# Sample's mixture heads: keys copied by residue inside each 512 tokens, local scores over a border in two pieces, prompt heads prepared one ahead

## The chip, the cores and the metric

The kernel runs on one core of a Trainium2 chip. The metric is device time in microseconds (us) of one execution, the median of several runs. PE is TensorE, DVE VectorE, ACT ScalarE, POOL GpSimd; SP (SyncE) issues nearly all DMAs here, in order, from one queue.

## The reference, cut to what matters

One encoder layer is run on two requests with shared weights, a prompt of 512 tokens and a sample of 1024, width 1024, all in float32. The part that the change touches is the token mixer's first eight heads ("mixture a"):

```python
qa, ka, va, qb, kb, vb = jnp.split(x @ w_in, splits, axis=-1)
qa = rotary(qa.reshape(B, T, 8, 64)); ka = rotary(ka.reshape(B, T, 8, 64))
oa = dilated_mixture_attention(qa, ka, va)   # windows (128, stride 1), (512, 4), (2048, 16), mixed by their lse
ob = neighbourhood_attention(qb, kb, vb, rpb)
y = concat([rms_norm(oa, g_mix_a), rms_norm(ob, g_mix_b)]) @ w_out
```

After it come cross-attention into 256 memory tokens and a squared-ReLU MLP, each with a residual sum and a layer norm.

## The kernel before, in words

Every float32 product is made of fp32r parts: a value is split in a high part and a rest, and a product takes three matmuls of up to 512 columns (`mm3`, L129 to L131).

The mixer's work is written as a list of 32 heads: eight a heads and eight b heads of the prompt, then eight a and eight b of the sample. A pair of heads shares its weights. A head is prepared by `qk_a` or `qk_b` for each 512 tokens (the group g): 24 matmuls project q and k into bank `pj`, DVE and POOL turn them (L383 to L386), ACT and DVE split them (L387, L388), and `stack` lays high and rest in the layout that the scores read, by SP's DMAs. The first head of a pair also projects v (24 matmuls for each group) and begins with the pair's weights, which SP loads (L92) and ACT and POOL split (L320, L321, L106, L107).

A prepared head is then attended in units of four blocks of 128 queries: the prompt has one unit a head, a sample a head four (two over near keys, two over every fourth key, "dilated"). `unit` is a generator of four steps: scores into bank `s` (L502, L503) with bias, maximum and exp on DVE and ACT; transposes of the probabilities (L528) and their split; the products with v into the one bank `o` (L544), which ACT empties (L550); the transposes back (L554). `push` puts a new unit in front and takes one step of each unit that is open, so four units overlap. `attend` walks the heads and hands out, between their units, the preparation of later heads: `lead(j)` is the head k during which head j is prepared, j - 2 for the prompt and j - 1 for the sample. What is written in this order a scheduler then places on each engine, so the instructions of neighbouring units and preparations stand mixed; `order`'s rows below are that final order.

For the sample's a heads, `stack` first writes k and q a second time, with the tokens sorted by their residue modulo 4, into a pair of tiles that all heads share (`env["perm"]`, tag `gb`; ACT L359 makes the high part, POOL L360 the rest). The next group's sort can begin when the DMAs that read the pair have landed. The head tile `hd` holds q as it is, k twice and q sorted, 1024 tokens each; k and the sorted q lie in four residue rows of 256 tokens, so a group of 512 tokens fills half of each row: a DMA moves four runs of 128 elements a partition (L368 to L370), a plain q one run of 512 (L366).

Layer norm of the sample's second 512 tokens (`ln_in` 8 to 11) with its load (L228), store (L230) and transposes (L137) stands with the first heads' preparation, ahead of the first `push`. `xs` is the layer-normed input in memory, `x0` (the prompt), `x1` and `x2` (the sample) are its parts as matmul operands.

Of the kernel before, what the change touches and what calls it, by code (L numbers as in the profile page):

```python
# [21 lines left out]
P = 128  # L22
# [9 lines left out]
def f32(ap):  # L32
    return ap.bitcast(F32)
# [3 lines left out]
def tile_encoder_layer(ctx: ExitStack, tc: tile.TileContext, d, outs):  # L37
    nc = tc.nc
    V, A, G, T, S = nc.vector, nc.scalar, nc.gpsimd, nc.tensor, nc.sync
# [21 lines left out]
    def slot(tag, n=None, dt=F32):  # L61
        w, bufs = SLOT[tag]
        t = sb.tile([P, w], dt, name=tag, tag=tag, bufs=bufs)
        return t if n is None else t[:, 0:n]
# [6 lines left out]
    def bank(tag):  # L71
        return ps.tile([P, 512], F32, name=tag, tag=tag, bufs={"t": 3, "o": 1}.get(tag, 2))
# [172 lines left out]
    z = slot("tok", 620)  # L245
# [3 lines left out]
    z = slot("tok", 465)  # L249
# [13 lines left out]
    call = lambda f, *a: (lambda: f(*a))  # L263
# [6 lines left out]
    def mixer(r, fill):  # L270
# [75 lines left out]
        def by_residue(a):  # L346
            return a.rearrange("p (x q) -> p q x", q=4)

        def residues(a):
            return a.rearrange("p (q x) -> p q x", q=4)  # L350

        def stack(hd, sh, sl, g):

            qs, k1, k2 = hd[0:3]
            tt = slice(g * 512, (g + 1) * 512)
            kh, kl = sh, sl
            if r:
                kh, kl = env["perm"]
                A.activation(residues(kh), by_residue(f32(sh)), AF.Copy)  # L359
                G.tensor_copy(residues(kl), by_residue(f32(sl)))  # L360
                kh, kl = residues(kh), residues(kl)
                k1, k2, qp = (residues(k)[:, :, g * P:(g + 1) * P] for k in hd[1:4])
            else:
                k1, k2 = k1[:, tt], k2[:, tt]
            for o, x, y, z in ((slice(0, 64), sh, kh, kl), (slice(64, P), sl, kl, kh)):
                S.dma_start(f32(qs[o, tt]), f32(x[0:P:2]))  # L366
                if r:
                    S.dma_start(f32(qp[o]), f32(y[0:P:2]))  # L368
                S.dma_start(f32(k1[o]), f32(y[1:P:2]))
                S.dma_start(f32(k2[o]), f32(z[1:P:2]))  # L370

        def head_tile(is_b):
            t = act.tile([P, 4096], F32R, name="hd", tag="act")
            return tuple(t[:, i * 1024:(i + 1) * 1024] for i in range(3 if is_b else 4))
# [95 lines left out]
        def unit(hd, v, h, blocks, norm=None, then=None, scale=1.0, local=False):  # L470
# [3 lines left out]
            qs, k1, k2 = hd[0:3]  # L474
# [3 lines left out]
            s, sx, pr, x = None, 512, None, 512  # L478
# [10 lines left out]
            for i, (q, kc, bias, n, lead, width, chunks) in enumerate(blocks):  # L489
                if sx + n > 512:  # L490
                    soften()
                    s, sx = bank("s"), 0
                if x + width > 512:
                    pr, x = slot("q", 512), 0
                so, p = s[:, sx:sx + n], pr[:, x + lead:x + lead + n]
                if lead:
                    G.memset(pr[:, x:x + lead], 0.0)
                if lead + n < width:
                    G.memset(pr[:, x + lead + n:x + width], 0.0)
                probs.append(pr[:, x:x + width])  # L500
                sx, x = sx + n, x + width
                T.matmul(so, q(qs), kc(k1), start=True, stop=False, skip_group_check=True)  # L502
                T.matmul(so, q(qs), kc(k2), start=False, stop=True, skip_group_check=True)  # L503
                todo.append((i, so, p, bias))
            soften()
            yield
# [16 lines left out]
            for pk in packs:  # L523
                t = bank("t")
                x = 0
# [9 lines left out]
            o = None  # L535
            for pk, (hi, lo) in zip(packs, split):
                if o is None:
                    o = bank("o")
                x = 0
                for c, u in pk:  # L540
                    n = len(u) * P
                    q0 = u[0][0] * P
                    for part in (hi, lo):
                        T.matmul(o[:, q0:q0 + n], v(c, h), part[:, x:x + n],  # L544
                                 start=(done == 0 and part is hi), stop=(done == total - 1 and part is lo),
                                 skip_group_check=True)
# [5 lines left out]
            t = bank("t").rearrange("p (i h e) -> p i h e", i=4, h=2)  # L552
# [20 lines left out]
        cols = lambda a, n, s=1: (lambda z: z[:, a:a + (n - 1) * s + 1:s])  # L573
# [5 lines left out]
        def attn_a1(hd, v, h, tab, hg):  # L579
            for j in range(2):  # L580
                bl = []
                for b in range(4 * j, 4 * j + 4):
                    lead, n = (64, 192) if b == 0 else (0, 192) if b == 7 else (0, 256)
                    k0 = (b * P - 64 + lead) // 4
                    bl.append((cols(b * P, P), lambda z, k0=k0, n=n: residues(z)[:, :, k0:k0 + n // 4],
                               tab[:, lead:lead + n], n, lead, 256, (b, (b + 1) % 8)))

                def then(raw, j=j):
                    S.dma_start(oas[0][j * 512:(j + 1) * 512, hg].rearrange("(i p) c -> p i c", p=P), raw)
                push(unit(hd, v, h, bl, then=then, local=True))  # L590
                yield
            for j in range(2):
                bl = []
                for q in (2 * j, 2 * j + 1):
                    for i in range(2):
                        bl.append((cols(q * 256 + i * P, P), cols(q * 256, 256),
                                   tab[:, 384 - P * i:640 - P * i], 256, 0, 256, (8 + 2 * q, 9 + 2 * q)))

                def then(raw, j=j):
                    for i in range(2):  # L600
                        S.dma_start(oas[1].rearrange("(h p q) g c -> q p h g c", p=P, q=4)[2 * j + i, :, :, hg],
                                    raw[:, 2 * i:2 * i + 2])
                push(unit((hd[3],) + hd[1:3], v, h, bl, then=then))
                yield
# [102 lines left out]

        return [x for is_b in (False, True) for pair in range(4) for x in pair_ab(pair, is_b)]

    def attend(heads, lead, after=()):  # L710

        for k, (_, units, n) in enumerate(heads):
            work = [f for j in range(len(heads)) if lead(j) == k for f in heads[j][0]]
            if k == len(heads) - 1:
                work += after
            us, done = units(), 0
            for i in range(n):
                next(us)
                while done < len(work) * (i + 1) // n:
                    work[done]()  # L720
                    done += 1
            for _ in us:
                pass
# [9 lines left out]
    def merge(t):  # L733
# [15 lines left out]
        for i in range(2):  # L749
# [2 lines left out]
        V.tensor_add(o, o, t[1][:, :, 0:64])  # L752
        S.dma_start(os_[1][rows, 0:512].rearrange("p (g c) -> p g c", g=8), o)

    plan = mixer(0, []) + mixer(1, [None] * 36 + [call(merge, t) for t in range(8)] +
                                [call(tok_load, 0, t) for t in range(4)])


# [162 lines left out]
            for f in extra.get((h, 1), ()):  # L921
                f()

    for f in plan[0][0] + [call(ln_in, 8)] + plan[1][0] + [call(ln_in, i) for i in range(9, 12)]:
        f()
    attend(plan, lambda j: j - 2 if j < 16 else j - 1, [call(y_tile, 0, t) for t in range(4)])
    while pipe:
        step()
    w_out_half(0, 0)
# [154 lines left out]
    for n, i in enumerate(UP):  # L1084
        _, what, into = PRODUCTS[i]
        xs_ = lefts.pop(n)
        for f in range(16):
# [3 lines left out]
            o = bank(("pj", "s", "t")[f % 3])  # L1091
# [9 lines left out]
            b = {2: (0, 1), 7: (1, 0), 6: (1, 1)}.get(i)  # L1101
# [176 lines left out]
```

## Time and profile before

| | |
|---|---|
| runs | 2379.81, 2386.12, 2386.31 us (median 2386.12) |
| the profiled execution | 2380.81 us, of which its trace spans 2379.0 |
| PE busy | 2284.5 us (96%), 11124 matmuls |
| DVE, ACT, POOL busy | 68%, 43%, 37% of the span |
| mean granted PE clock | 0.990 |

In the trace the prompt's heads run from about 134 to 345 us, the sample's a heads to about 650, its b heads and the rest of the mixer's end to about 990, the cross-attention and the MLP up to 2379. PE works in the order of its own queue, so a matmul whose operand is late holds all behind it; an idle stretch of PE carries the name of what ended it.

### The profile page before, as it was taken

What the parts mean: (1) busy time and instruction counts of PE and PEld (TensorE: products, weight loads), DVE (VectorE), ACT (ScalarE), POOL (GpSimd) and SP (SyncE); (2) the same over time, 40 slices, a digit from 0 to 9 for tenths busy, and PEclk for the clock granted to TensorE, in tenths of its full rate; (3) what the DMA queues carried; (4) which work ended last, traced back from release to release, by engine and by line L of the source; (5) the groups of instructions that cost most, each with busy time, mean ns of one, the idle gap of its engine ahead of it and who ended that gap; (6) DMA issues with size and microseconds to landing.
All of it is one profiled execution on the core that took longest, in us unless ns stands there. A gap on an engine that the chain in (4) does not pass through costs nothing. (4 is left out here: it accounts for less than half of the span.)

```text
span 2379.0 us, 33108 instructions
## 1 busy us (share of the span) xinstructions
PE 2284.5 (96%) x11124; PEld 1892.7 (80%) x11124; DVE 1608.6 (68%) x3297; ACT 1022.7 (43%) x2176; POOL 879.3 (37%) x820
## 2 busy tenths in 40 slices
PE   8989998999999999999999999999999999999997
PEld 6868777888888787777878877878888888887875
DVE  6265635677656667668676487767776696689786
ACT  4345645666555532334333333333354322344541
POOL 7564443223324211433154355555541314310221
PEclk9999999999999999999999999999999999999998
DMA  9675345677535642435335444344489999974781
GB/s 318 201 228 146 78 117 121 137 137 150 116 95 135 180 124 92 133 115 176 117 107 185 121 155 147 120 139 147 149 223 221 210 222 250 224 177 156 165 206 68
DMA packets 410235, 375.21 MB, mean 158 GB/s; under 512 B 72513, under 2 KB 326481, under 8 KB 410065
## 3 DMA queue, kind: packets, MB, share of 16 engines
q1 hardware_dynamic: 367056, 339.54, 49.7%
q0 software_dynamic: 43008, 33.56, 10.1%
q8 instruction: 88, 1.44, 0.3%
q14 instruction: 83, 0.67, 0.1%
HBM read 290.76 MB, written 52.98 MB: 144 GB/s over the span
## 5 line engine op out<-in xcount | busy, mean ns | idle before, releaser
L107 POOL TENSOR_TENSOR wl<-wraw,wh 128x512 fp32r<-128x512 f32 x80 | 106.2, 1344 | 218.5 <-ACT wh L106 169.3
L1062 ACT ACTIVATE wh<-q 128x512 fp32r<-128x512 f32 x176 | 110.1, 626 | 140.5 <-DMA q<-in_w_up_dram 61.5
L486 ACT ACTIVATE q<-q,st 128x256 f32<-128x256 f32 (+3 forms) x256 | 138.4, 544 | 60.3 <-DVE st L485 59.0
L1063 DVE TENSOR_TENSOR wh<-q,wh 128x512 fp32r<-128x512 f32 x176 | 125.8, 717 | 54.2 <-ACT wh L1062 53.9
L321 POOL TENSOR_TENSOR wl<-wraw,wh 128x256 fp32r<-128x256 f32 x128 | 94.0, 757 | 160.3 <-ACT wh L320 144.9
L1047 POOL DMA_DIRECT2D q<-in_w_up_dram x64 | 83.3, 1416 | 181.0 <-DVE h L1100 72.8
L532 DVE TENSOR_TENSOR pt<-t,pt 128x512 fp32r<-128x512 f32 x160 | 105.2, 670 | 54.8 <-ACT pt L531 54.0
L1047 POOL DMA_DIRECT2D q<-in_w_down_dram x64 | 56.4, 921 | 218.9 <-DVE wraw L1134 92.9
L1000 POOL TENSOR_TENSOR wl<-pt,wh 128x512 fp32r<-128x512 f32 x64 | 91.6, 1451 | 118.6 <-ACT wh L999 118.4
L544 PE MATMUL o<-pt,tok 128*128 128x256 f32 (+3 forms) x576 | 116.1, 315 | 9.1 <-ACT q L550 8.6
L531 ACT ACTIVATE pt<-t 128x512 fp32r<-128x512 f32 x160 | 89.6, 579 | 80.1 <-PE o L544 76.4
L107 POOL TENSOR_TENSOR wl<-qt,wh 128x512 fp32r<-128x512 f32 x64 | 101.6, 1608 | 51.3 <-ACT wh L106 43.4
L1013 DVE TENSOR_TENSOR tok<-tok,t 128x512 f32<-128x512 f32 x124 | 82.9, 680 | 37.5 <-PE t L131 37.4
L1013 DVE TENSOR_TENSOR tok<-tok,s 128x512 f32<-128x512 f32 x124 | 83.8, 679 | 29.7 <-PE s L131 29.4
L131 PE MATMUL pj<-x20h,wl 128*128 128x512 f32 x256 | 101.4, 396 | 2.5 <-POOL wl L107 2.3
L119 POOL TENSOR_TENSOR wl<-wraw,wh 128x512 fp32r<-128x512 f32 x48 | 64.7, 1366 | 103.7 <-ACT wh L118 103.7
L129 PE MATMUL pj<-x20h,wh 128*128 128x512 f32 x256 | 100.6, 393 | 1.0 <-ACT wh L106 0.9
L528 PE MATMUL t<-ident,q 128*128 128x128 f32 x624 | 97.9, 276 | 3.3 <-ACT q L486 1.8
L158 POOL TENSOR_TENSOR lnst<-lnst,mhalf 128x1 f32<-128x1 f32 x44 | 54.2, 1234 | 124.7 <-DVE lnst L157 124.6
L130 PE MATMUL pj<-x20l,wh 128*128 128x512 f32 x256 | 100.2, 391 | 0.0
L544 PEld LDWEIGHTS o<-pt,tok 128*128 128x128 f32 x576 | 85.0, 192 | 16.5 <-ACT q L550 11.3
L999 ACT ACTIVATE wh<-pt 128x512 fp32r<-128x512 f32 x64 | 36.9, 624 | 121.7 <-PE s L131 103.2
(497 smaller groups left out, 7527.9 us busy)
## 6 DMA issues: line engine op xcount, KB each, us to landing
q<-in_w_up_dram SPq DMA_DIRECT2D x128, 256.0 KB
q<-in_w_down_dram SPq DMA_DIRECT2D x128, 256.0 KB
wraw<-in_w_in_dram SPq DMA_DIRECT2D x96, 256.0 KB
qt<-in_w_up_dram SPq DMA_DIRECT2D x32, 512.0 KB
pt<-in_w_down_dram SPq DMA_DIRECT2D x32, 512.0 KB
q<-in_w_up_dram POOLq DMA_DIRECT2D x64, 256.0 KB, 8.1
q<-in_w_down_dram POOLq DMA_DIRECT2D x64, 256.0 KB, 5.9
sa<-kv SPq DMA_DIRECT2D x28, 512.0 KB
```

The source lines that it names most:

```text
L107: G.tensor_sub(wl[:, sl], r, f32(wh[:, sl]))
L129: T.matmul(out, lh[k], rh[k], start=(k == 0), stop=False, skip_group_check=True)
L130: T.matmul(out, lh[k], rl[k], start=False, stop=False, skip_group_check=True)
L131: T.matmul(out, ll[k], rh[k], start=False, stop=(k == n - 1), skip_group_check=True)
L486: A.activation(p, p, AF.Exp, bias=nm, scale=scale, accum_out=den)
L528: T.transpose(t[:, x:x + P], p, ident)
L532: V.tensor_sub(lo[:, 0:x], t[:, 0:x], f32(hi[:, 0:x]))
L544: T.matmul(o[:, q0:q0 + n], v(c, h), part[:, x:x + n], start=(done == 0 and part is hi), stop=(done == total - 1 and part is lo), skip_gro ...
L1013: V.tensor_add(x, x, q)
L1047: G.dma_start(out, src, accum_op=ADD)
L1062: A.activation(dst[0], x, AF.Copy)
L1063: low.tensor_sub(dst[1], x, f32(dst[0]))
```

## The change

Four edits.

- In `stack` the sorted k and q of a group stay together: each group fills one run of 512 elements a partition, residue by residue inside it. k's copies are issued ahead of q's.
- A local block of the sample reads keys from 64 tokens ahead of its 128 queries to 64 behind. Blocks 3 and 4 of each head reach over token 512, where the layout now breaks, so their scores are made in two pieces: 48 and 16 keys of each residue. Each piece has its own matmuls (for k1 and for k2).
- A dilated block reads its 128 queries as one run, its keys as two runs of 128.
- `attend` prepares every head during the one ahead of it, and `ln_in` 8 to 11 becomes the filling of the prompt's first pushes (`fill`, after a first empty place).

```diff
         def stack(hd, sh, sl, g):
 
-            qs, k1, k2 = hd[0:3]
+
             tt = slice(g * 512, (g + 1) * 512)
+            qs, k1, k2 = (a[:, tt] for a in hd[0:3])
             kh, kl = sh, sl
             if r:
                 kh, kl = env["perm"]
                 A.activation(residues(kh), by_residue(f32(sh)), AF.Copy)
                 G.tensor_copy(residues(kl), by_residue(f32(sl)))
-                kh, kl = residues(kh), residues(kl)
-                k1, k2, qp = (residues(k)[:, :, g * P:(g + 1) * P] for k in hd[1:4])
-            else:
-                k1, k2 = k1[:, tt], k2[:, tt]
             for o, x, y, z in ((slice(0, 64), sh, kh, kl), (slice(64, P), sl, kl, kh)):
-                S.dma_start(f32(qs[o, tt]), f32(x[0:P:2]))
-                if r:
-                    S.dma_start(f32(qp[o]), f32(y[0:P:2]))
                 S.dma_start(f32(k1[o]), f32(y[1:P:2]))
                 S.dma_start(f32(k2[o]), f32(z[1:P:2]))
+                S.dma_start(f32(qs[o]), f32(x[0:P:2]))
+                if r:
+                    S.dma_start(f32(hd[3][o, tt]), f32(y[0:P:2]))
...
-                T.matmul(so, q(qs), kc(k1), start=True, stop=False, skip_group_check=True)
-                T.matmul(so, q(qs), kc(k2), start=False, stop=True, skip_group_check=True)
+                for dst, keys in kc if local else [(lambda z: z, kc)]:
+                    T.matmul(dst(so), q(qs), keys(k1), start=True, stop=False, skip_group_check=True)
+                    T.matmul(dst(so), q(qs), keys(k2), start=False, stop=True, skip_group_check=True)
...
-                    k0 = (b * P - 64 + lead) // 4
-                    bl.append((cols(b * P, P), lambda z, k0=k0, n=n: residues(z)[:, :, k0:k0 + n // 4],
-                               tab[:, lead:lead + n], n, lead, 256, (b, (b + 1) % 8)))
+                    kc, k0, end = [], b * P - 64 + lead, b * P - 64 + lead + n
+                    for g in range(2):
+                        x0, x1 = max(k0, 512 * g) // 4, min(end, 512 * g + 512) // 4
+                        if x0 < x1:
+                            kc.append((lambda z, a=x0 - k0 // 4, e=x1 - k0 // 4: residues(z)[:, :, a:e],
+                                       lambda z, g=g, a=x0 - P * g, e=x1 - P * g:
+                                       residues(z[:, 512 * g:512 * g + 512])[:, :, a:e]))
...
-                        bl.append((cols(q * 256 + i * P, P), cols(q * 256, 256),
+                        bl.append((cols(512 * i + q * P, P),
+                                   lambda z, q=q: z.rearrange("p (g x) -> p g x", g=2)[:, :, q * P:(q + 1) * P],
...
-    def attend(heads, lead, after=()):
+    def attend(heads, after=()):
 
         for k, (_, units, n) in enumerate(heads):
-            work = [f for j in range(len(heads)) if lead(j) == k for f in heads[j][0]]
-            if k == len(heads) - 1:
-                work += after
+            work = heads[k + 1][0] if k + 1 < len(heads) else after
...
-    plan = mixer(0, []) + mixer(1, [None] * 36 + ...
+    plan = mixer(0, [None] + [call(ln_in, i) for i in range(8, 12)]) + mixer(1, [None] * 36 + ...
...
-    for f in plan[0][0] + [call(ln_in, 8)] + plan[1][0] + [call(ln_in, i) for i in range(9, 12)]:
+    for f in plan[0][0]:
         f()
-    attend(plan, lambda j: j - 2 if j < 16 else j - 1, [call(y_tile, 0, t) for t in range(4)])
+    attend(plan, [call(y_tile, 0, t) for t in range(4)])
```

The scheduler's order changes with it. On PE the rows are the same up to the 511th and from about the 4,280th of some 10,070 on (from about 138 to 990 us of the trace); between them 25 rows more stand in another order. Lines of the changed kernel are 2 to 3 lower in `stack` and `unit`: L363 and L364 copy k, L365 and L367 q, L500 and L501 make scores, L406 and L454 transposes of v, L526 of probabilities.

The first place is PE at the first a head of the sample (`hd_3552`). `s_3756` holds the scores of blocks 2 and 3, of which block 3 is the first to read keys of the second 512 tokens; `pj_3693` is the projection of v for the second 512 tokens, 24 matmuls. Before:

```order
L457 MATMUL pj_3684<-ident_92,kv_3676 128x128 x4
L554 MATMUL t_3798<-ident_92,q_3508 128x128 x2
L528 MATMUL t_3839<-ident_92,q_3744 128x128 x3
L502 MATMUL s_3756<-hd_3552 128x256
L503 MATMUL s_3756<-hd_3552 128x256
L502 MATMUL s_3814<-hd_3552 128x256
...
L503 MATMUL s_3814<-hd_3552 128x256
L129 MATMUL pj_3693<-x2h_1141,wh_3641 128x512
L130 MATMUL pj_3693<-x2l_1142,wh_3641 128x512
```

And now, with 24 rows of `pj_3693` between the two parts:

```order
L500 MATMUL s_3756<-hd_3552 128x4x48
L501 MATMUL s_3756<-hd_3552 128x4x48
...
L500 MATMUL s_3816<-hd_3552 128x4x16
L501 MATMUL s_3816<-hd_3552 128x4x16
L526 MATMUL t_3843<-ident_92,q_3744 128x128
L129 MATMUL pj_3693<-x2h_1273,wh_3641 128x512
...
L131 MATMUL pj_3693<-x2h_1273,wl_3642 128x512
L500 MATMUL s_3756<-hd_3552 128x4x16
L501 MATMUL s_3756<-hd_3552 128x4x16
```

Before, the scores over the second group's keys stood ahead of v's projection; now only the pieces over the first group's keys do, and the piece over the second group's (4x16) stands behind it.

The second place is SP's queue at the start of the prompt's heads: `wraw` is a half of pair 1's weights, `tok_1143` the sample's tokens for `ln_in` 8, `tok_1209` and `tok_1235` those for 9 and 10, `tok_1026` and `tok_1027` tiles of the prompt's second head. Before:

```order
L370 DMA tok_1026<-qt_1084 64x512
L228 DMA tok_1143<-in_x_sample_dram 128x1024
L380 DMA kv_1194<-in_c_rope_dram 128x2x512
L92 DMA wraw_1337<-in_w_in_dram 128x4x128
L92 DMA wraw_1343<-in_w_in_dram 128x4x128
...
L230 DMA xs1_58<-tok_1143 128x1024
L366 DMA tok_1026<-qt_1196 64x512
...
L228 DMA tok_1209<-in_x_sample_dram 128x1024
L228 DMA tok_1235<-in_x_sample_dram 128x1024
```

And now:

```order
L365 DMA tok_1025<-qt_1084 64x512
L377 DMA kv_1196<-in_c_rope_dram 128x2x512
L92 DMA wraw_1321<-in_w_in_dram 128x4x128
L92 DMA wraw_1327<-in_w_in_dram 128x4x128
...
L92 DMA wraw_1671<-in_w_in_dram 128x4x128
L363 DMA tok_1027<-qt_1198 64x512
L364 DMA tok_1027<-qt_1198 64x512
```

The loads and stores of `ln_in` have left the place; weights stand there, also a first load of pair 2 (`wraw_1671`), ahead of the second head's copies.

## Rows read from the trace of the kernel before

**Rows 1.** The page, busy time of each engine, share of the span, instructions.

```profile
PE 2284.5 (96%) x11124; PEld 1892.7 (80%) x11124; DVE 1608.6 (68%) x3297; ACT 1022.7 (43%) x2176; POOL 879.3 (37%) x820
```

**Rows 2.** Windows by stage: stretch, its us, busy by engine, PE clock, DMA.

```profile
134.00:180.00 46.00, 38.51 (x175) 29.70 (x175) 36.74 (x73) 24.35 (x50) 31.08 (x26) 0.93 0.78 233
180.00:345.00 165.00, 157.17 (x827) 130.06 (x827) 85.92 (x268) 98.13 (x251) 78.43 (x113) 0.99 0.44 111
345.00:650.00 305.00, 287.93 (x1758) 252.63 (x1757) 200.79 (x655) 182.96 (x499) 89.21 (x118) 0.98 0.64 133
650.00:990.00 340.00, 327.49 (x1722) 277.57 (x1722) 224.56 (x588) 158.18 (x359) 99.68 (x113) 0.99 0.45 126
```

**Rows 3.** PE's waits, 345 to 650: us in total, times, longest us.

```profile
PE s L502 <- DMA hd<-gb: 9.3, 5, 5.6
PE o L544 <- ACT q L550: 4.9, 3, 1.9
```

**Rows 4.** PE's waits, 134 to 180.

```profile
PE t L137 <- POOL tok L173: 2.6, 2, 1.7
PE pj L129 <- ACT wh L106: 1.4, 1, 1.4
PE pj L129 <- ACT wh L320: 1.3, 1, 1.3
```

**Rows 5.** PE's waits, 180 to 345.

```profile
PE o L544 <- ACT q L550: 3.3, 3, 2.7
```

**Rows 6.** Windows at a low granted clock (0.50, third number from the end).

```profile
141.00:144.40 3.40, 3.40 (x9) 2.64 (x8) 0.55 (x1) 2.30 (x6) 3.40 (x3) 0.50 0.60 189
164.90:168.30 3.40, 3.40 (x13) 2.90 (x13) 2.89 (x9) 3.40 (x8) 3.40 (x5) 0.50 0.88 282
380.40:383.40 3.00, 2.94 (x10) 2.65 (x11) 2.10 (x9) 0.00 (x0) 0.00 (x0) 0.51 0.20 51
```

**Rows 7.** Timelines of PE, ACT and SP at the sample's first head.

```profile
363.53 0.39 PE L131 MATMUL pj<-x2h,wl 128*128 128x512 f32 x1
363.76 0.39 PE L129 MATMUL pj<-x1h,wh 128*128 128x512 f32 x1
...
370.86 1.13 ACT L359 ACTIVATE gb<-qt 128x512 fp32r<-128x512 f32 x1 [2.77 <-DMA hd<-gb]
...
376.25 0.61 SPq L369 DMA_DIRECT2D hd<-gb  x1
...
380.46 0.58 PE L502 MATMUL s<-hd 128*128 128x256 f32 x1 [5.61 <-DMA hd<-gb]
```

**Rows 8.** Timelines of SP and PE at a b head: L402 copies 64x1024.

```profile
821.82 0.47 SPq L402 DMA_DIRECT2D hd<-hd  x1
...
825.12 0.57 PE L502 MATMUL s<-hd 128*128 128x256 f32 x2 [0.87 <-DMA hd<-hd]
```

**Rows 9.** Timelines of SP and PE at the sample's second head.

```profile
422.12 0.62 SPq L369 DMA_DIRECT2D hd<-gb  x1
...
427.16 0.36 PE L502 MATMUL s<-hd 128*128 128x256 f32 x1 [1.37 <-DMA hd<-gb]
```

**Rows 10.** Timeline of PE: starts of scores of 256 and 192 columns.

```profile
388.15 0.28 PE L503 MATMUL s<-hd 128*128 128x256 f32 x1
388.27 0.25 PE L502 MATMUL s<-hd 128*128 128x192 f32 x1
388.36 0.28 PE L503 MATMUL s<-hd 128*128 128x192 f32 x1
```

**Rows 11.** Timelines of SP and ACT: pair 1's second half of weights.

```profile
131.62 1.09 SPq L92 DMA_DIRECT2D wraw<-in_w_in_dram  x2
...
137.30 1.64 ACT L320 ACTIVATE wh<-wraw 128x256 fp32r<-128x256 f32 x4 [8.36 <-DMA wraw<-in_w_in_dram]
```

**Rows 12.** Timelines of PE and SP: a prompt b head's projection and last copy.

```profile
347.86 0.39 PE L131 MATMUL pj<-x0h,wl 128*128 128x512 f32 x1
...
352.24 0.52 SPq L403 DMA_DIRECT2D tok<-tok  x1
```

More of the change, by code (lines that the diff above doesn't have):

```diff
@@ L583, in attn_a1 @@
                     lead, n = (64, 192) if b == 0 else (0, 192) if b == 7 else (0, 256)
-                    k0 = (b * P - 64 + lead) // 4
-                    bl.append((cols(b * P, P), lambda z, k0=k0, n=n: residues(z)[:, :, k0:k0 + n // 4],
-                               tab[:, lead:lead + n], n, lead, 256, (b, (b + 1) % 8)))
+                    kc, k0, end = [], b * P - 64 + lead, b * P - 64 + lead + n
[5 more added lines that the diff above has]
+                                       residues(z[:, 512 * g:512 * g + 512])[:, :, a:e]))
+                    bl.append((cols(b * P, P), kc, tab[:, lead:lead + n], n, lead, 256,
+                               (b, (b + 1) % 8)))
                 def then(raw, j=j):
@@ L753, in merge @@
         S.dma_start(os_[1][rows, 0:512].rearrange("p (g c) -> p g c", g=8), o)
-    plan = mixer(0, []) + mixer(1, [None] * 36 + [call(merge, t) for t in range(8)] +
+    plan = mixer(0, [None] + [call(ln_in, i) for i in range(8, 12)]) + mixer(1, [None] * 36 + [call(merge, t) for t in range(8)] +
                                 [call(tok_load, 0, t) for t in range(4)])
```

## The prediction

> **What bounds the kernel now.** I read the page's busy times first: PE works 96% of the span [rows 1], so only what PE waits for, how fast its clock runs and how many matmuls it has can change the time. Then the windows by stage, to see where PE is not busy. The two built programs have PE's same rows up to about 138 us and again from about 990 us, so all that can move lies in the four stages of [rows 2]: there PE is idle 7.5 us of 46, 7.8 of 165, 17.1 of 305 and 12.5 of 340. That is 45 us in all, and no edit can win more than that and what the clock loses beside it.
>
> The waits tell whose idle time it is. In the sample's a heads 9.3 us of the 17.1 end with a copy of keys into the head tile, five waits, one of 5.6 [rows 3]; the next, 4.9, is bank `o` waiting for ACT to empty it, which no edit touches by itself. At the start of the prompt's heads PE waits 2.6 us for the layer norm of the sample's second half, and 2.7 for split weights [rows 4]; in that stretch DVE is busy 36.7 and POOL 31.1 of 46 us and the DMA engines 0.78, the highest share of the four [rows 2]. In the rest of the prompt the largest wait is bank `o` again [rows 5].
>
> The clock is the last view. It fell to 0.50 (1.2 of 2.4 GHz) in three stretches of these stages that the change can reach [rows 6]. A stretch of 3.4 us in which PE worked at half speed cost 1.7 us, twice; the third held 2.94 us of work, 1.5 us lost. Each came within or right after waits of PE: the last behind the 5.6 us.
>
> **The copies by residue.** At the sample's first head the projection of q and k for the second 512 tokens ends at about 363.8, and the scores that read its keys begin at 380.46, held for 5.61 us: 16.7 us from projection to keys [rows 7]. Part of it is the shared pair of tiles: ACT's sort of the second group begins at 370.86, after 2.77 us of waiting for the first group's copies to land. Then the last copy is issued at 376.25 and lands 4.2 us later. At the second head the last copy takes 5.0 us (422.12 to 427.16) [rows 9]. These copies are of 512-byte runs. The nearest row of long runs is a b head's copy of 64x1024, twice the bytes in 4 KB runs: 821.82 to 825.12, 3.3 us [rows 8]. So a landing should come 0.9 to 1.7 us sooner, and it lies on the path twice, once before the sort and once before the scores: 1.8 to 3.4 us of 16.7, of which I take 2.6. The lower bound is nothing.
>
> What PE does meanwhile matters as much. I counted the rows between the end of the second group's projection and the first score over its keys, at the start-to-start times of the trace: 0.23 us for 512 columns [rows 7], 0.12 for 256 [rows 10], 0.11 for a transpose. Before, the eight heads have 10.1, 16.5, 23.3, 16.5, 23.3, 16.5, 23.3, 16.5 us of PE work there; now 15.5, 16.2, 24.1, 14.7, 15.3, 15.6, 15.9, 14.9. The first head gains because 24 matmuls of v (5.5 us) stand ahead of the waiting piece now. Its 5.6 us become about 1.2: 16.7 less 15.5, or by the other view a transpose that now stands 1.5 us behind its scores where it stood 2.2 before. The other four waits share 3.7 us (9.3 less 5.6), so the second heads of a pair needed about 16.5 + 0.9 = 17.4 us. With 2.6 less they need 14.8, and 16.2, 14.7, 15.6 and 14.9 leave next to nothing; I take 1.0 for all. So 9.3 us become 2.2, and the clock's 1.4 us behind the long wait come back: **8.5 us less**. SP still issues eight copies a group at about 0.6 us each, so nothing is won or lost in the queue; which copy comes first is worth at most two places, 1.3 us, and is inside the 2.6.
>
> A rule of the Trainium skill speaks against this part: DMA: Bandwidth & Descriptors, section "Why small descriptors are slow (HBM only)", says that transfers from SBUF to SBUF do not suffer from small descriptors. By it the landings stay at 4.2 to 5.0 us; that is the first rival below. The rows so far differ from it (3.3 us for twice the bytes in long runs), though at another moment with other traffic.
>
> **Two pieces.** Eight heads, two blocks each, two matmuls each: 32 matmuls more, for the same columns. A 192-column score takes 0.09 us start to start, a 256-column one 0.12 [rows 10]; 64 columns lie between 0.03, their share, and the 0.11 of a 128-column transpose. So a piece more costs nothing to 0.08 us; I take 0.06, nearer to the upper end as 192 columns already cost more than their share of 256: **1.9 us more** (0 to 2.6). The dilated blocks have as many matmuls of the same size as before.
>
> The Trainium skill, TensorE: Matmul & The Clock Gate, section "LDWEIGHTS (loading the stationary operand)", makes a weight load a matter of its 128 columns, whatever follows; by its 1.2 columns a ns an estimate of 0.107 us a piece and 3.4 us for 32 would replace the 1.9. The 0.09 us of the 192-column rows is below that.
>
> **Layer norm into the pushes.** `ln_in` 8 to 11 loads, stores and transposes leave the stretch from 134 to 180. Pair 1's weights were issued at 131.62, behind the first of those loads, and ACT could split them at 137.30 [rows 11]; they come a place earlier now and share the DMA engines with less. The stretch loses 7.5 us idle and 3.4 us clock now, 10.9 in all. I do not expect all of it: the layer norms' own 2.6 us move to eight later places of four transposes, half of it kept (1.3); of the 2.7 for weights and 1.0 for their rests 1.4; of the remaining 1.2 us 0.4. New is that the second head's scores stand 13.4 us of PE work behind their projection instead of 18.6, and the first load of pair 2 stands ahead of its copies in SP's queue: 1.6. That keeps 4.7 us idle and one slow stretch, 6.4: **4.5 us less**. Bounds: 9 less when the place runs clean, 5 more when the second and third head both wait for their copies.
>
> **Prompt heads one ahead.** The same matmuls in another order; what was prepared two units ahead hides a longer chain. For a b head the projection ends at 348.1, the last copy is issued at 352.24 [rows 12], and with 3.3 us to land [rows 8] the scores can begin 7.5 us after the projection. In the new order the six closest b heads have 7.3 to 8.8 us of PE work there (before 7.9 to 14.4, without a wait). So the cover is just enough. If it is gone each such head pays the difference. Bank `o`'s waits (3.3 and 4.9 us) stay: the units' closest products stand 1.0 to 2.0 us of work apart in both orders. For this and for all else that stands in another order I take **2.0 us more**, with 3 less and 6 more as bounds.
>
> **Sum.** -8.5 + 1.9 - 4.5 + 2.0 = -9.1 us. Against the profiled execution's own 2380.8 us that is 2371.7. The median of the runs is 5.3 us above that execution and the lowest run 1.0 below; I add half of the 5.3: **2374 us**.
>
> **Rivals.**
> 1. The copies land no sooner. Then the four second heads wait 17.4 less 16.2, 14.7, 15.6 and 14.9, 8.2 us, and the first head 1.2: 9.4 in place of the 2.2. The sum is -1.9: 2381. For it: all copies share one queue and 16 DMA engines with weights, 0.64 busy [rows 2]. Against: [rows 8]. Chance 0.2.
> 2. The start of the prompt gives nothing: what `ln_in` did to DVE, POOL and DMA there it does somewhat later. -4.6: 2379. For it: the work is the same. Against: from 180 to 345 DVE is busy only 86 of 165 us and the DMA engines 0.44 [rows 2], so there is room. Chance 0.15.
> 3. Slower: the b heads of the prompt wait for their own copies. It decides from a chain of 9.5 us on. At 10.5, 3 us over what [rows 12] and [rows 8] give, six heads with about 8.1 of cover wait 2.4 each, 14 us, and two slow stretches add 3.4: -9.1 + 17.8, less the 2.0 already in the sum, +6.7, so 2390. For it: the six covers are all within 1.3 us of the chain. Against: in the trace no prompt head waited for a copy, one of them at a cover of 7.9. Chance 0.1.
>
> The forecast keeps 0.55, its own range 2366 to 2380. About 0.3%, 7.2 us, is what a measurement can tell from no change. Faster by more than that: most of the forecast, 0.53. Within: the rest of it, rivals 1 and 2, 0.36. Slower: rival 3, 0.11. The range that holds 8 in 10 takes in rivals 1 and 2 and part of the way to 3: 2364 to 2387.
>
> **What would show it.** Right: in the sample's a heads PE's wait for `hd<-gb` falls from 9.3 to some 2 us and no slow stretch stands near 380; copies L363 to L367 land within 3.5 us; 32 score matmuls more, each some 0.06; fewer waits for weights and layer norm between 134 and 180. Wrong: landings above 4 us; waits of `s` for `tok<-tok` or `tok<-qt` copies in the prompt; L137 still waiting for POOL, later; ACT's emptying of `o` held longer.

## The result, and the profile after

The changed kernel took 2361.18 us (median of four runs, 2356.64 to 2364.81) against 2385.12 before (2379.81 to 2386.31): ratio 0.9903, 95% interval 0.9878 to 0.9928. That is 24 us, or 17 to 29, less, where 12 were forecast, and 2.8 us under the lower end of the range. Its profiled execution took 2364.81 us (of which its trace spans 2363.0), 16.0 less than the one before. It lies 3.6 above the median of its kernel; the one before lies 4.3 below the median of its own.

The page's busy times, after. PE has 32 matmuls more than in [rows 1] and about the same busy time:

```profile
PE 2283.9 (97%) x11156; PEld 1891.7 (80%) x11156; DVE 1602.6 (68%) x3297; ACT 1023.0 (43%) x2176; POOL 882.3 (37%) x820
```

Windows by stage, after, with the columns of [rows 2], and the stretch near 380:

```profile
134.00:180.00 46.00, 42.35 (x200) 34.12 (x199) 30.21 (x69) 24.90 (x56) 27.64 (x26) 0.96 0.70 206
180.00:345.00 165.00, 157.69 (x837) 129.91 (x836) 92.37 (x275) 100.17 (x251) 83.65 (x116) 0.98 0.44 120
345.00:650.00 305.00, 297.09 (x1826) 259.94 (x1826) 206.48 (x679) 189.26 (x511) 92.11 (x120) 1.00 0.55 136
...
376.50:383.40 6.90, 6.18 (x51) 5.66 (x49) 5.44 (x22) 6.06 (x20) 1.54 (x3) 1.00 0.57 165
```

Beside [rows 2], PE's idle time fell from 7.5 to 3.7 us in the first stretch, stayed in the second (7.8, 7.3) and fell from 17.1 to 7.9 in the sample's. PE's waits from 345 to 650, after:

```profile
PE o L542 <- DVE st L482: 1.3, 2, 0.8
...
PE s L500 <- DMA hd<-qt: 0.4, 1, 0.4
PE s L500 <- DMA hd<-gb: 0.3, 1, 0.3
...
PE o L542 <- ACT q L548: 0.2, 1, 0.2
```

Against [rows 3] the copies' 9.3 us are 0.7, where 2.2 were forecast, and the 4.9 of bank `o` behind ACT are 0.2, which was not forecast at all. From 134 to 180 the waits for weights and layer norm of [rows 4] have given place to one for the second head's copies:

```profile
PE s L500 <- DMA tok<-qt: 3.3, 2, 2.5
```

The clock stood at 1.00 near 380, where [rows 6] has 0.51.

Stretches that hold the same work are a better measure than equal times. I cut both traces at the first projection of a prompt head, the first score of a sample head, and two matmuls at whose places the programs are alike again, so the four rows are the prompt's heads, the sample's, the mixer's end and the rest. Before:

```profile
113.60:370.32 256.72, 239.38 (x1226) 196.56 (x1224) 142.49 (x381) 141.80 (x343) 127.49 (x161) 0.98 0.54 144
370.32:696.98 326.66, 309.59 (x1870) 271.40 (x1869) 212.31 (x696) 196.19 (x533) 90.19 (x119) 0.98 0.59 122
696.98:1058.70 361.72, 345.67 (x1796) 289.69 (x1795) 243.47 (x607) 159.19 (x356) 113.31 (x121) 0.99 0.46 135
1058.70:2379.00 1320.30, 1286.39 (x5770) 1048.85 (x5768) 959.19 (x1537) 477.02 (x865) 473.19 (x363) 1.00 0.64 167
```

After:

```profile
113.49:367.90 254.41, 241.32 (x1237) 198.34 (x1235) 140.59 (x382) 144.03 (x347) 128.67 (x162) 0.97 0.52 145
367.90:685.46 317.56, 309.58 (x1889) 270.76 (x1890) 210.72 (x696) 194.94 (x530) 89.86 (x117) 1.00 0.51 125
685.46:1045.65 360.19, 344.80 (x1796) 288.48 (x1795) 243.81 (x608) 158.95 (x356) 115.98 (x122) 1.00 0.47 136
1045.65:2363.00 1317.35, 1284.23 (x5770) 1048.00 (x5768) 955.86 (x1536) 476.46 (x865) 473.05 (x362) 1.00 0.63 167
```

The prompt's heads lose 2.3 us, the sample's 9.1, the mixer's end 1.5 and the rest 3.0. (By the sample's first score 11 matmuls more are done now, so 2 to 3 us of the sample's 9.1 belong to the prompt.) The last two are mostly not the edits'. In the rest the PE order is the same, and over the 19 traces of this record that stretch lasts 1314 to 1320 us, with the one before near the upper end. At the mixer's end the trace before has 6.8 us at half clock from 909, with 6.0 of PE's work in them, and the one after 3.4 us from 814: 1.3 us of the 1.5.

### The profile page after: what moved, and what is told of

The parts are those of the page before. It is cut to its first block, busy times and chain, and to the rows that moved or that the text cites. A ratio compares the mean times of both kernels' runs of the same rounds, so it can differ in the third digit from the quotient of the medians.

```text
span 2363.0 us, 33140 instructions
## 1 busy us (share of the span) xinstructions
PE 2283.9 (97%) x11156; PEld 1891.7 (80%) x11156; DVE 1602.6 (68%) x3297; ACT 1023.0 (43%) x2176; POOL 882.3 (37%) x820
## 5 line engine op out<-in xcount | busy, mean ns | idle before, releaser
L526 PE MATMUL t<-ident,q 128*128 128x128 f32 x624 | 97.9, 277 | 4.0 <-DVE pt L530 1.9
```

The source lines that it names most:

```text
L526: T.transpose(t[:, x:x + P], p, ident)
```

## Experiments

Each was timed in rounds beside the kernel before, whose median was 2382.2 to 2383.5 in every set; the intervals of the ratios are 0.1 to 0.2% to either side, so a few us between two variants settle nothing. All edits but that of the short runs also make the scheduler place hundreds of PE's rows anew, so a difference is that of an edit with its new order.

**Which part.** Theory A: the gain is the copies'. Theory B: it is the new order of preparation. Theory C: it is what the scheduler happens to put ahead of bank `o`'s emptying. First, the layout alone (with pieces, k's copies first):

```diff
-    attend(plan, [call(y_tile, 0, t) for t in range(4)])
+    attend(plan, lambda j: j - 2 if j < 16 else j - 1, [call(y_tile, 0, t) for t in range(4)])
...
-    for f in plan[0][0]:
+    for f in plan[0][0] + [call(ln_in, 8)] + plan[1][0] + [call(ln_in, i) for i in range(9, 12)]:
```

> The layout with its pieces alone; heads prepared two ahead in the prompt and the layer norms up front, as before. Theory A (the gain lies in the sample's a heads: their copies are fewer packets, and v's projection covers the first wait): that stage (PE's rows from the first sample projection to its last a product) loses 9 to 11 us as in the changed kernel, with the wait for hd<-gb under 2 us; the kernel stands 9 to 16 us under the one before. Theory B (the new order of preparation makes the gain): at most 4 us under. Theory C (what the scheduler places ahead of ACT's emptying of bank o decides, 4.9 us of waits, and it falls another way with every edit): waits of o for L548/L550 between 0 and 5 us, whatever the layout.

Measured: 2372.03 us, ratio 0.9958 (0.9943 to 0.9972), 10.4 us less than 2382.4. Then the order alone, the same lines as in the change on the kernel before:

> Heads one ahead and the layer norms in the pushes alone; the layout of before, no pieces. Theory A: the sample's a heads keep waits of 8 to 10 us for hd<-gb, and the kernel stands 0 to 4 us under the one before. Theory B: 10 us or more under. Theory C: as for the layout alone, the waits of o move by up to 5 us either way.

Measured: 2367.38 us, 0.9936 (0.9919 to 0.9953), 15.0 less. The changed kernel again, on the same chip:

> The changed kernel as it is, beside the three others on one chip, since its four times lie 8 us apart. If the trace's 16 us are the whole, it stands 14 to 18 us under the kernel before; if the medians' 24 us are, 22 to 26.

Measured: 2361.18 us, 0.9910 (0.9891 to 0.9928), 21.2 less. The order is worth 10.8 beside the new layout, the layout 6.2 beside the new order.

What the halves did to PE's waits from 345 to 650, where [rows 3] has 9.3 us for `hd<-gb` and 4.9 for bank `o`. The layout alone:

```profile
PE s L500 <- DMA hd<-gb: 1.7, 2, 0.9
...
PE o L542 <- ACT q L548: 0.5, 1, 0.5
```

The order alone, with copies in runs of 512 bytes as before:

```profile
PE o L544 <- ACT q L550: 1.9, 2, 1.4
PE s L502 <- DMA hd<-gb: 1.5, 2, 1.1
```

Theory A asked for 8 to 10 us of copies' waits to stay with the order alone, and 1.5 stayed; it asked for 9 to 11 us to go from the sample's stretch with the layout alone, and 5.0 went (326.66 to 321.67). So A is refuted as the only cause, though B's bound for the layout alone, 4 us, is passed as well. Theory C is not set aside: in each of the 18 other traces the copies' waits there sum to at most 2.5 us and bank `o`'s behind ACT to at most 1.9. What the kernel before loses there belongs to its one order, and every other order tried sheds most of it.

The layout alone also shows what the order did at the sample's first head. Its PE timeline there still has v's projection behind the scores over the second 512 tokens, and PE waits twice:

```profile
377.07 0.27 PE L500 MATMUL s<-hd 128*128 128x64 f32 x1 [2.09 <-DVE tok L408]
...
378.56 0.42 PE L500 MATMUL s<-hd 128*128 128x64 f32 x1 [0.72 <-DMA hd<-gb]
```

The first of these is put down to DVE, but DVE's signal came at 376.79. The weight load ahead of this score also waits for q's plain copy, which SP issued at 373.61 (L365) and whose last signal came at 376.98; the load began at 377.04. Block 4's queries belong to the second 512 tokens, so its piece over the first keys needs their q, which is now copied after k.

**The size of the runs.** The changed kernel, with high part and rest woven in their pair of tiles, so that a copy is four runs of 512 bytes again; PE's order is the same row for row.

```diff
-                    env["perm"] = parts("gb") if r and not is_b else None
+                    env["perm"] = [z[:, :, c:c + P] for z in [slot("gb", dt=F32R).rearrange("p (q x) -> p q x", q=4)] for c in (0, P)] ...
...
-                S.dma_start(f32(k1[o]), f32(y[1:P:2]))
+                S.dma_start(f32(residues(k1[o])), f32(y[1:P:2]))
```

> The changed kernel, but the sorted k and q lie woven in their pair of tiles (four runs of 128 of the high part, each followed by one of the rest), so that every copy of them is again four 512-byte packets a partition in place of one of 2 KB; PE's order is the same row for row. Theory A1 (size of the packets): landings go back to 4.3 us and more and PE waits 4 to 7 us more for them, so 4 to 10 us slower than the changed kernel. Theory A2 (it was what stands between projection and scores): the landings grow, but less than 2 us of it reach PE; the time is that of the changed kernel within 3 us.

Measured: 2367.40 us, 0.9940 (0.9922 to 0.9958), 6.2 more than the changed kernel, which is in A1's range. The view of DMA queues from 345 to 650 (packets, MB, share of 16 engines' time), changed kernel:

```profile
q1 hardware_dynamic: 55690, 41.11, 54.1%
```

With short runs:

```profile
q1 hardware_dynamic: 73266, 41.28, 64.3%
```

A copy of each, from SP's issue to POOL's next sort that waits for it, changed kernel (3.8 us):

```profile
477.62 0.59 SPq L367 DMA_DIRECT2D hd<-gb  x1
...
481.41 1.12 POOL L361 CAST gb<-qt 128x512 fp32r<-128x512 f32 x1 [2.48 <-DMA hd<-gb]
```

With short runs (4.7 us):

```profile
481.49 0.61 SPq L367 DMA_DIRECT2D hd<-gb  x1
...
486.21 1.12 POOL L361 CAST gb<-qt 128x512 fp32r<-128x512 f32 x1 [3.21 <-DMA hd<-gb]
```

Over the copies `hd<-gb` of the stretch whose landing released an instruction, the median from issue to release is 4.46 us before (43 copies), 3.73 after (28) and 4.48 with short runs (31); with the layout alone it is 3.82, with the order alone 4.45. So the landing follows the size of the runs in either order. How much of it reaches PE is less clear. PE's waits for copies from 345 to 650, short runs:

```profile
PE s L500 <- DMA hd<-gb: 1.7, 2, 1.2
...
PE s L500 <- DMA hd<-qt: 0.7, 2, 0.5
```

That is 1.7 us more than the 0.7 after, by A2's bound of 2 and not the 4 to 7 of A1. The sample's stretch is 2.4 us longer than in the first profile of the changed kernel and 3.8 than in the second; the prompt's is 2.8 and 3.2 longer, with half clock for 10.2 us from 149.9, where no sorted copy runs yet, against 3.4 us from 151.7 and 151.2 there. So the size of the runs is worth some 2 to 4 us, and the rest of the 6.2 is not shown to be its.

**Which part of the order.** One ahead with the layer norms up front (`for f in plan[0][0] + [call(ln_in, i) for i in range(8, 12)]`, no filling), and two ahead with the layer norms in the pushes, both with the new layout:

> The new layout and heads one ahead, but the layer norms 8 to 11 up front. The order part of the change was worth 11 us on top of the layout (2372.0 to 2361.2). Theory L (the layer norms' going makes it, in the prompt's first 50 us): the time goes back to 2368 to 2372. Theory O (one ahead makes it: it puts v's projection between the sample's first keys and their scores, and lets the weights come in earlier): 2360 to 2365, and no stretch at half clock near 380. Half each: about 2366.

> The new layout and the layer norms in the prompt's pushes, but the prompt's heads prepared two ahead as before. Theory L: 2359 to 2364, with the waits for the layer norm gone between 134 and 180 us. Theory O: 2368 to 2372, with a wait of 2 us or more at the sample's first scores over its second 512 tokens and half clock behind it.

Measured: 2373.14 us (0.9960, 0.9945 to 0.9975) and 2372.61 (0.9963, 0.9949 to 0.9977). Neither theory L nor O: each half alone gives nothing over the layout's 2372.03, both together 11. So I varied from which head on the preparation goes one ahead, with the layer norms up front:

```diff
-    attend(plan, lambda j: j - 2 if j < 16 else j - 1, ...
+    attend(plan, lambda j: j - 2 if j < 15 else j - 1, ...
```

> The new layout, layer norms up front, heads two ahead, but the prompt's last head is prepared one ahead, so that the last head but one has a preparation beside it again. In the built program this alone puts v's 24 matmuls of the second 512 tokens ahead of the sample's first scores over them. Theory V (that place is what one ahead is worth: with the layout alone PE waited 2.8 us there, 2.7 for bank o at 340, and three stretches at half clock followed, 5.1 us): 6 to 9 us under the layout alone, 2363 to 2366. Theory S (the order's 11 us come from the start of the prompt): 2370 to 2374.

Measured: 2371.59 us, 0.9949 (0.9937 to 0.9962). Theory V, that v's place is what counts, fell: v's projection stood where I wanted it, and the wait moved to the pieces ahead of it (2.00 us at 374.98), again for q's copy (issued at 371.33, last signal at 374.89). With 8, and later 12, in place of 15:

> The new layout, layer norms up front, heads 1 to 7 two ahead and all after them one ahead: the start of the kernel before with the rest of the changed one. Theory V: as the run before this, 2362 to 2367, and the b heads' covers of 7 to 9 us suffice. Theory S: 2370 to 2374. If one ahead costs the b heads something (the third rival of the prediction), it stands 3 us or more above the run with only the last head moved.

> The new layout, layer norms up front, one ahead only from head 12 on (the last two b pairs). With the layout alone the time was 2372.0, with one ahead from 8 on 2362.7, with the last head alone 2371.6. If each b pair gives its share, this stands near 2367; if it all comes at the prompt's end (bank o at 340, the sample's first scores, the clock behind them), near 2363; if it comes from where a heads give over to b heads, near 2371.

Measured: 2362.73 us (0.9917, 0.9903 to 0.9932) and 2364.05 (0.9926, 0.9904 to 0.9947). Against the layout alone, the last four b heads bring 8.0 of the 9.3 us, the last one alone 0.4. The same number (8) in the kernel before, and with the layer norms in the pushes:

> The layout of before, layer norms up front, one ahead from head 8 on: one number of the kernel before changed. If the gain of one ahead doesn't need the layout, 8 to 14 us under the kernel before (2369 to 2375); if its point is to let the pieces wait behind v, at most 4 us under.

> The new layout, layer norms in the 2nd to 5th push, heads 1 to 7 two ahead, the others one ahead. If the layer norms' move gains by itself, 2357 to 2361; if it only makes up for what one ahead costs the a heads, 2361 to 2366; if with two heads ahead it costs as in the run with all two ahead (waits of 1 to 3 us at 150, 201, 220, 230), 2364 to 2370.

Measured: 2374.32 us (0.9966, 0.9949 to 0.9983), 9.2 under 2383.5, so the gain doesn't need the layout; and 2368.00 (0.9929, 0.9912 to 0.9947), so the layer norms' move gains nothing there. Together, with the new layout:

| heads one ahead | layer norms up front | in the pushes |
|---|---|---|
| none of the prompt's | 2372.0 | 2372.6 |
| 15 | 2371.6 | |
| 12 to 15 | 2364.1 | |
| 8 to 15 | 2362.7 | 2368.0 |
| all | 2373.1 | 2361.2 (the change) |

What the b heads gain shows in the traces of the layout alone and of 12 to 15. ACT at the prompt's end, layout alone, and PE beside it:

```profile
338.42 0.74 ACT L320 ACTIVATE wh<-wraw 128x256 fp32r<-128x256 f32 x2 [1.19 <-DMA wraw<-in_w_in_dram]
...
339.63 0.59 ACT L548 ACTIVATE q<-o 128x512 f32<-128x512 f32 x1
...
340.28 1.55 PE L542 MATMUL o<-pt,tok 128*128 128x256 f32 x8 [2.68 <-ACT q L548]
```

Its windows, with the clock (third number from the end):

```profile
313.50:316.90 3.40, 3.40 (x13) 2.96 (x12) 1.88 (x15) 1.95 (x9) 3.15 (x7) 0.50 0.44 88
340.80:344.20 3.40, 3.40 (x17) 3.40 (x17) 1.06 (x6) 2.01 (x10) 3.40 (x7) 0.50 0.44 94
378.40:385.20 6.80, 6.64 (x24) 5.97 (x25) 3.24 (x14) 2.83 (x10) 0.00 (x0) 0.50 0.33 84
```

With heads 12 to 15 one ahead the split L320 stands behind the emptying, PE waits 1.18, and the clock is whole:

```profile
338.95 0.60 ACT L548 ACTIVATE q<-o 128x512 f32<-128x512 f32 x1
339.42 0.76 ACT L320 ACTIVATE wh<-wraw 128x256 fp32r<-128x256 f32 x2
...
339.60 1.15 PE L542 MATMUL o<-pt,tok 128*128 128x256 f32 x8 [1.18 <-ACT q L548]
```

Its windows near 340 and 380:

```profile
340.80:344.20 3.40, 3.01 (x14) 2.39 (x14) 1.11 (x7) 3.19 (x12) 3.40 (x6) 1.00 0.21 54
376.00:380.00 4.00, 3.39 (x24) 2.95 (x23) 2.50 (x12) 2.32 (x7) 1.53 (x3) 1.00 0.26 60
```

In the layout alone PE's waits of 0.3 us and more from 305 to 386 sum to 8.0 us, and the stretches at 0.50 cost an estimated 6.7 more, half of PE's work in them; here the waits sum to 3.3 and no stretch is slow. That is 11.4 for 8.0 measured, from one execution each. The clock's part holds in the other traces: all five with heads 12 to 14 two ahead have half clock near 340 and again near 380. Of the fourteen with these heads one ahead, three have it near 340, three others between 366 and 374, and eight at neither place.

What one ahead costs the a heads while the layer norms stand up front I did not find. With all heads one ahead, PE's largest waits from 134 to 180 are 2.7 us for the layer norm and 2.0 for split weights, no longer than in [rows 4]. Three half-clock stretches lie between 129 and 160, 10.2 us, but the run with 8 has 10.2 us of them between 127 and 168. The traces of the two lie 12.9 us apart, spread over the prompt (4.8), the sample's heads (2.8), the mixer's end (2.3) and what is outside them.

**Bank o and the weights.** In the kernel before, each of the four long waits for bank `o` has this on ACT: the split of the next pair's weights, late by its DMA, ahead of L550 (ACT, then PE):

```profile
455.85 1.60 ACT L320 ACTIVATE wh<-wraw 128x256 fp32r<-128x256 f32 x4 [1.36 <-DMA wraw<-in_w_in_dram]
457.35 1.05 ACT L531 ACTIVATE pt<-t 128x512 fp32r<-128x512 f32 x2
458.30 0.59 ACT L550 ACTIVATE q<-o 128x512 f32<-128x512 f32 x1
...
458.94 0.38 PE L544 MATMUL o<-pt,tok 128*128 128x256 f32 x1 [1.94 <-ACT q L550]
```

To test it, POOL made the high part too, in the kernel before and in the changed one:

```diff
-                        A.activation(dh, src, AF.Copy)
+                        G.tensor_copy(dh, src)
                         G.tensor_sub(dl, src, f32(dh))
```

> The kernel before, with the high part of w_q and w_k made by POOL (in front of its own subtraction) in place of ACT. If ACT's split, held up by its DMA, is what keeps bank o occupied, the four waits of 1.5 to 2.7 us for L550 (338.87, 458.94, 524.61 and 589.56) fall to about 1 us each or less, the half-clock stretches at 339 and 591 go too, and the time falls by 4 to 9 us. Against it: POOL's split is late and PE waits for wl instead, 0 to 5 us more. If the bank is kept by something else, the waits stay and the time with them.

> The same edit on the changed kernel, where the waits for L548 are only 2.6 us in all. By the theory of the split at most 2 us to gain, and up to 5 to lose to POOL: 2359 to 2366.

Measured: 2376.11 us (0.9971, 0.9959 to 0.9984), 6.1 less than the kernel before and inside the range expected, and 2370.31 (0.9952, 0.9932 to 0.9971), 9.1 more than the changed one, beyond what was expected. In the first no wait for bank `o` is left from 345 to 650, and 0.7 us in two from 180 to 345. But the copies' wait has gone from 9.3 us to 0.5 as well, though copies and layout are those of the kernel before:

```profile
PE pj L409 <- ACT kv L445: 2.3, 1, 2.3
...
PE s L502 <- DMA hd<-gb: 0.5, 1, 0.5
```

Compared by names and shapes, some 1,550 of PE's 11,124 rows, from 116 to 857 us, stand in another order than before. So the 6.1 us can't be put down to the bank, and that the split kept it rests on the four places in the trace before. Nor is a late split enough: in the layout alone L320 waits 2.11 us for its weights at 582.93, the emptying follows at 586.85, and PE waits 0.54. The slow stretch near 339 did not go either: half clock lasted from 336 to 350. Why the edit costs the changed kernel 9.1 us is not shown; some 1,900 of PE's rows moved there.

**Order of the copies, place of the layer norms.** q's copies ahead of k's in all a heads, in the prompt alone, and with heads 8 to 15 one ahead:

> The changed kernel with q's copies issued ahead of k's again, in all a heads. Both profiles of the changed kernel hold a wait of 2.5 to 3.6 us of the prompt's second head for its last copy, q's, near 151 us; the order alone, with q first, has 0.9 there and a prompt stage shorter by 3 to 4.7 us. If the order of the copies is what costs this, the time falls by 2 to 5 us, to 2356 to 2359; if it is only where the scheduler put the scores, it stays within 2 us; if k first is worth something at the sample's heads, it rises by up to 3.

> The changed kernel with q's copies first in the prompt alone. If q first helps the prompt and k first the sample's heads, this is the fastest, 2355 to 2358; if the copies' order doesn't matter, 2359 to 2363; if q first in all heads is as fast, k first in the sample is worth nothing.

> One ahead from head 8 on with the new layout, and q's copies ahead of k's again. If the copies' order is worth nothing, 2361 to 2365; if k first helps the sample's heads, 2365 to 2368; if q first helps the second a head of the prompt, 2358 to 2361.

Measured: 2360.33 us (0.9910, 0.9895 to 0.9924), 2363.98 (0.9925, 0.9911 to 0.9939) and 2362.56 (0.9913, 0.9895 to 0.9930): the order of the copies can't be told from nothing. The layer norms in the 7th to 10th push:

```diff
-    plan = mixer(0, [None] + [call(ln_in, i) for i in range(8, 12)]) + mixer(1, ...
+    plan = mixer(0, [None] * 6 + [call(ln_in, i) for i in range(8, 12)]) + mixer(1, ...
```

> The changed kernel with the layer norms 8 to 11 in the 7th to 10th push of the prompt in place of the 2nd to 5th. If what they cost lies in the heads around them (waits of 2.5 to 3.6 us at 151 for the second head's copy, which share the queue with them), the time falls to 2356 to 2360; if they are hidden in both places, it stays at 2359 to 2363; if they now delay the b heads' weights and tables, up to 2366.

Measured: 2377.76 us, 0.9974 (0.9964 to 0.9984), 16.6 more than the changed kernel and outside what was expected. The largest of PE's waits from 180 to 345:

```profile
PE t L526 <- DVE pt L530: 4.9, 2, 4.7
PE o L542 <- ACT q L548: 4.1, 4, 2.2
```

So where the layer norms stand among the pushes matters more than whether they are in the pushes at all (12.0 against all heads one ahead with them up front). No variant is measurably faster than the changed kernel.

## Why the prediction was wrong

**The failed step** is "Prompt heads one ahead", priced at 2.0 us more with 3 less as its bound. One ahead from head 8 on is worth 9.3 us less with the new layout and 9.2 less with the old one; together with the layer norms' move it is worth 10.8 less, where -4.5 and +2.0 gave 2.5 less. I asked only whether the b heads' copies would still be covered. They are: no wait for `tok<-tok` stands among PE's waits of the prompt, so the third rival is refuted. I did not ask what else the old order made PE wait for. With heads 12 to 15 one ahead, against the layout alone, the wait for bank `o` near 340 falls from 2.7 to 1.2 us and those at the sample's first scores from 2.8 to 1.2, and the half clock near 340 and 380 is gone. That clock was in the sum only for the 380: the trace before is slow near 339, 592 and 909 too, which [rows 6] leaves out.

**"Bank `o`'s waits stay"** is a sentence of that step which failed too, for the most part not by that step. I looked at the distance between two units' products on PE and not at ACT's queue, where the emptying stood behind a split that waited for its weights. Of the 8.2 us [rows 3, 5] 2.6 are left behind ACT. The sample's 4.9 fell to 0.5 with the layout alone; of the prompt's 3.3 there are 2.4 left, and one ahead only shortened the longest. The sum had this at nothing.

**The copies.** The landing came 0.7 us sooner, just under the 0.9 to 1.7 expected, and short runs take it back. Layout and pieces were forecast at 6.6 less; they gave 10.4 alone and 6.2 beside the new order. But it is luck in part that the size came out so near: the copies' 9.3 us fell to 1.5 with the order alone, in runs of 512 bytes, and the layout's gain alone holds bank `o`'s 4.4. So the forecast wait went, but the sooner landing was not needed for most of it; in the changed order it is worth 1.7 us of PE's waits (0.7, and 2.4 with short runs). By the Trainium skill (DMA: Bandwidth & Descriptors, "Why small descriptors are slow (HBM only)") copies inside SBUF should not suffer from short runs. The 4.48 and 3.73 us differ from it, and the measurement decides.

**The first head** was credited to the layout alone, since v's projection stood ahead of the waiting piece in the changed order. With the layout alone v stays behind, 2.8 us of waits remain, most of them for q's copy that the prediction didn't ask about, and half clock follows (378.4 to 385.2). With the order alone PE waits for no copy there; 1.9 us remain ahead of the first scores, with 3.4 us of half clock behind them. So either edit shortens the wait, and its 5.6 us can't be given to one of them.

**The pieces** were forecast at 0.06 us each, 1.9 in all. A cut block and an uncut one in the changed kernel's trace (queries shared by all matmuls of a block):

```profile
376.83 0.19 PE L500 MATMUL s<-hd 128*128 128x64 f32 x1
376.86 0.28 PE L501 MATMUL s<-hd 128*128 128x64 f32 x1
376.97 0.34 PE L500 MATMUL s<-hd 128*128 128x192 f32 x1
...
377.25 0.30 PE L500 MATMUL s<-hd 128*128 128x256 f32 x1
...
377.51 0.39 PE L526 MATMUL t<-ident,q 128*128 128x128 f32 x2
```

The cut one takes 0.42 us from its first start to the next block's, the uncut one 0.26; of the seven cut blocks that stand in one piece four take 0.42 and three 0.51. So a matmul more costs 0.08 to 0.12 us there, an estimated 2.6 to 3.9 for 32: over the forecast, and at its bound of 2.6 or over it. By the Trainium skill (TensorE: Matmul & The Clock Gate, "LDWEIGHTS (loading the stationary operand)") an estimate of 0.107 us a piece stood against the 0.06; the blocks measured agree with it better, though single starts lie closer (0.03 us at 376.83).

**The layer norms.** -4.5 was forecast for the move as such. It is worth 0.6 us more with all heads two ahead, 5.3 more with heads 8 to 15 one ahead (intervals that overlap), and 12.0 less with all one ahead. The forecast of the stretch itself, 4.7 us idle and one slow stretch, was close (3.7, one at 151.7), but the second head's wait for its copies was twice the 1.6 forecast (3.3). What was wrong was to price the two edits apart and add them.

**The sum** of 2371.7 stood 6.9 us above the profiled 2364.8. Adding half of the 5.3 us between execution and median took it 2.3 further up, and the changed kernel's median lies 3.6 under its own profile. These make the 12.8 between 2374 and 2361.2. Three runs of the kernel before were known then, 2379.8 to 2386.3; later sets reach from 2372.9 to 2390.5, a spread that the range had no room for.

Open is why one ahead from the first head on, against from the eighth, costs 10.4 us with the layer norms up front and gains 6.8 with them in the pushes.

## What to carry to other kernels

Where engines work in order, look on each for an instruction that waits for a DMA and stands ahead of one that frees a scarce buffer; what it costs depends on how soon the buffer is wanted again (1.9 us at one place here, 0.5 at another). Two edits of the order of work can each be worth nothing and together 11 us, so neither their prices nor single experiments may be added up; time the corners. And a wait that goes with an edit need not have gone by the edit's own mechanism: look whether it goes with the other edits too.

## What the runs showed of the hardware

Copies inside SBUF of the same 128 KB took 4.48 us in runs of 512 bytes and 3.73 in runs of 2 KB (medians from issue to release, 31 and 28 copies), with the same order on PE. And a short wait may or may not be followed by half clock. With 1.18 us for bank `o` and 0.4 to 0.5 for the next projection, 1.8 us later, the granted clock stayed at 1.00 in the runs with heads 12 to 15 (above), with 8 to 15 and with q's copies first. In both profiles of the changed kernel the same two waits were followed by 0.50. PE's timeline in the second:

```profile
337.11 0.62 PE L542 MATMUL o<-pt,tok 128*128 128x256 f32 x3 [1.18 <-ACT q L548]
```

The window behind it:

```profile
338.90:342.30 3.40, 3.33 (x8) 2.67 (x9) 0.78 (x8) 3.05 (x12) 3.10 (x5) 0.50 0.20 50
```
